# A hybrid decoder trunk: one pool per kind of tile, the second tokens' factors in the order of their products, and memory loaded earlier

## Chip, cores and metric

One NeuronCore of one Trainium2 chip runs the whole program in one launch. The metric is device time in microseconds (us) of that core. PE is TensorE, DVE VectorE, ACT ScalarE, POOL GpSimd, SP SyncE; in the rows a `q` behind an engine's name is its queue, where it issues DMAs or waits.

## What is computed

Two decoder layers over 512 tokens of width 1024, in float32, each of four steps with a layer norm (LN) behind every one. Layer 0 mixes with differential attention, layer 1 with a causal pooling mixer; both attend to 256 memory tokens.

```python
for i in range(DEPTH):                       # DEPTH = 2, a = 4 ** 0.25
    x = layer_norm(a * x + 0.5 * swiglu_ffn(x, ffn_w_in[i, 0], ffn_w_out[i, 0]), ...)
    h = diff_attention(x, ...) if i == 0 else pool_mixer(x, ...)
    x = layer_norm(a * x + h, ...)
    x = layer_norm(a * x + memory_cross_attention(x, mem, xa_wq[i], xa_wkv[i], xa_wo[i]), ...)
    x = layer_norm(a * x + 0.5 * swiglu_ffn(x, ffn_w_in[i, 1], ffn_w_out[i, 1]), ...)

def swiglu_ffn(x, w_in, w_out):              # D = 1024, D_FF = 2816
    g, u = jnp.split(x @ w_in, 2, axis=-1)
    return (jax.nn.silu(g) * u) @ w_out
```

In differential attention the output of a head is o = (p0 - lam p1) v, then scaled by the inverse root of its mean square plus a small constant; p0 and p1 are two softmaxes.

## The kernel before

Tokens lie in four tiles X of 128. Every float32 operand is split into a high and a low part: ACT casts the high one (`split`, line 111), DVE subtracts it for the low one (line 112), and `mm3` (lines 172 to 174) makes each product of three matmuls, hi x hi, hi x lo, lo x hi. Split weights are tiles wh (ACT) and wl (DVE) in the pool w; raw weights are loaded by SP into ra and rc (FFN) or raw (the other stages, two buffers).

An FFN multiplies 2x2 blocks with seven products instead of eight. `up` handles 256 of the 2816 columns of a half: its products x, y, z, then z and x again, use the factors of x in the order 0, 1, 3, 6, 4, 5, 2. Three such lanes run side by side in the first turn (`FFN_TURNS`), and two with a `down` beside them in the others. `more` (line 533) adds a further block to a raw tile by an accumulating DMA that POOL issues. Factors 0 and 1 are the transposed first 256 tokens, 2 to 6 are made from all 512: `turn_factors` (line 487) turns tokens 2 and 3 by PE and makes, a token at a time, s1 to s4 and the splits of factors 2 to 6 by half-width operations; the two sums of line 454 give it the first tokens back in one piece. `ffn` (line 427) traces it between the first x product and the y products.

Each stage ends with `to_tokens` or, in an FFN, `plain_down`: eight products over (half, token) in the order `LAST` (line 48), of which `summed` adds each to X and starts the LN of a token when its second half is in (`ln_token`, line 331: square on ACT, two small steps on POOL, two steps on DVE, lines 353 and 355). `TURNS` names the products behind which a finished token is already transposed for the next stage. The weights of `to_tokens` go to wh and wl, or, where `homes` is given, to activation tiles that have come free.

Each stage opens its pools anew: w, raw and one pool named phase for all activation tiles; six PSUM banks are a pool too (aux). A tile in a new pool waits for those older tiles whose addresses it covers. What the tile framework's scheduler puts in which order on an engine follows the order of tracing, unless `issue_after` or `high_priority` says otherwise. In differential attention `weave` (line 177) mixes the main stream (projections) with the side stream (scores, turns and outputs of heads); `da_out` (line 897) ends a head with four squares on ACT and five small steps on POOL. `load_memory` (line 1107) loads the memory into a raw tile, transposes it by 16 small matmuls and splits it; in layer 0 that is traced when cross-attention begins.

Of the kernel before, what the change touches and what calls it, by code (L numbers as in the profile page):

```python
# [17 lines left out]
P = 128  # L18
# [29 lines left out]
LAST = ((0, 0), (0, 1), (1, 0), (1, 1), (0, 2), (0, 3), (1, 2), (1, 3))  # L48
TURNS = ((0, 3), (1, 2))
# [52 lines left out]
class Trunk:  # L102
# [18 lines left out]
    def act(self, tag, shape=(P, S), dtype=F32R):  # L121

        return self.phase.tile(list(shape), dtype, tag=tag, name=tag, bufs=self.bufs[tag])
# [3 lines left out]

    @contextmanager
    def phase_pool(self, gain, spare, **bufs):

        self.gain, self.spare = gain, spare
        with self.tc.tile_pool(name="phase", bufs=1, reuse_waits="tile") as p:
            self.phase, self.bufs = p, bufs
            yield

    @contextmanager
    def stage_pools(self, raw, aux, w=5, order=("w", "raw")):


        pool = lambda name, **k: self.tc.tile_pool(name=name, bufs=1, reuse_waits="tile", **k)  # L140
        with ExitStack() as ctx:
            pools = {n: ctx.enter_context(pool(n)) for n in order}
            self.wp, self.rawp = pools["w"], pools["raw"]
            self.memp = pools.get("mem")
            self.auxp = ctx.enter_context(pool("aux", space=PSUM))
            self.w_bufs, self.raw_bufs, self.aux_bufs, self.aux_turn = w, raw, aux, 0
            yield

    def raw_tile(self, shape, tag="raw"):
        return self.rawp.tile([P] + list(shape), F32, tag=tag, name=tag, bufs=self.raw_bufs[tag])  # L150
# [4 lines left out]
    def aux(self, name, tag=None):  # L155
        if tag is None:
            tags = [t for t in self.aux_bufs if t != "yz"]
            tag = tags[self.aux_turn % len(tags)]
            self.aux_turn += 1
        return self.auxp.tile([P, S], F32, tag=tag, name=name, bufs=self.aux_bufs[tag])  # L160
# [55 lines left out]
    def hl(self, shape):  # L216
        return (
            self.wp.tile(shape, F32R, tag="wh", name="wh", bufs=self.w_bufs),
            self.wp.tile(shape, F32R, tag="wl", name="wl", bufs=self.w_bufs),
        )  # L220
# [110 lines left out]
    def ln_token(self, t):  # L331
# [20 lines left out]
        for i, c in enumerate(cols):  # L352
            nc.vector.scalar_tensor_tensor(y[i], X[:, c], mean, g[i], ALU.add, ALU.mult)
# [4 lines left out]
        self.ends.append((square, end))  # L358
        if t == NT - 1:
# [24 lines left out]
    def turn(self, t, half, two_pass=None):  # L384

        pt = self.aux("pt", "px" if "px" in self.aux_bufs else None).rearrange("p (c n) -> p c n", c=4)
# [8 lines left out]
        self.turned = self.split(hi[:, :, o], lo[:, :, o], pt)  # L395

# [30 lines left out]
    def ffn(self, layer, j, ln, beside=None):  # L427
# [22 lines left out]
        raw = [self.tmp("hb", (P, 4, 2 * P)) for _ in range(2)]  # L450
        act, dve = self.first_split
        with self.tc.issue_after(act.ins), self.tc.issue_after(dve.ins):
            for r, (hi, lo) in zip(raw, self.factors):
                self.nc.vector.tensor_tensor(r, hi.bitcast(F32), lo.bitcast(F32), ALU.add)
            self.turn_factors(2, raw)
        for w in works[1:]:
            next(w)
        self.turn_factors(3, raw)
        n = len(FFN_TURNS)
        for turn in range(n):  # L460
            behind = turn == n - 1
            for step in range(1 if turn == 0 else 0, 9 if behind else 7):
                if step == 4:
# [23 lines left out]
    def turn_factors(self, t, raw):  # L487


        nc, F = self.nc, self.factors  # L490
        o = slice(t % 2 * P, (t % 2 + 1) * P)
        pts = []
        for half in range(2):
            pt = self.aux("pt", (("py", "yz"), ("px", "py"))[t % 2][half])
            pt = pt.rearrange("p (c n) -> p c n", c=4)
            with self.behind():
                self.transpose4(pt, [self.X[t][:, half * S + j * P : half * S + (j + 1) * P] for j in range(4)])
            pts.append(pt)
        a11, a12 = (r[:, :, o] for r in raw)
        a21 = self.tmp("sr", (P, 4, P))  # L500
        nc.scalar.copy(a21, pts[0])
        s12, s34 = (self.tmp(f"b{i}", (P, 2, 4, P)) for i in ((1, 2) if t == 2 else (3, 4)))
        s1, s2, s3, s4 = s12[:, 0], s12[:, 1], s34[:, 0], s34[:, 1]
        part = lambda i, x: self.split(F[i][0][:, :, o], F[i][1][:, :, o], x)
        nc.vector.tensor_tensor(s1, pts[1], a21, ALU.subtract)
        part(3, s1)
# [358 lines left out]
    def da_scores(self, st, i):  # L865
# [4 lines left out]
        mx, sm, cf = self.small("mx"), self.small("sm"), self.small("cf", (P, 1))  # L870
        rc = st["rc"][:, i]
# [12 lines left out]
        nc.vector.reciprocal(rc, sm)  # L884
        nc.vector.scalar_tensor_tensor(cf, sm[:, 0:1], self.nlam, rc[:, 1:2], ALU.mult, ALU.mult)
# [11 lines left out]
    def da_out(self, st, i):  # L897
        nc = self.nc
        if i == 0:
            st["o"] = self.tmp("o", (P, NT, P))  # L900
# [480 lines left out]
```

## Time and profile before

| | us |
|---|---|
| median of 3 runs (lowest, highest) | 2035.2 (2034.3, 2036.3) |
| the profiled execution | 2036.3 |
| its span, first to last instruction | 2034.5 |
| busy in it: PE, DVE, ACT, POOL | 1966.0, 1575.2, 1019.3, 324.7 |

The stages follow one another in the span: FFN (0 to 345), differential attention (to 608), cross-attention (to 782), FFN (to 1132), FFN (to 1477), pooling mixer and cross-attention (to 1683), FFN (to the end). The profile page says how busy each engine is; a view of windows gives that for chosen stretches, with the clock granted to PE (1.00 is 2.4 GHz); a list of waits says who waited for whom; a timeline gives single instructions.

### The profile page before, as it was taken

The numbers are of one execution on the slowest core, as the hardware profiler recorded it, in microseconds if no ns is written. First come the engines' busy times: TensorE is split into PE (matmuls) and PEld (weight loads), VectorE is DVE, ScalarE is ACT, GpSimd is POOL, SyncE is SP. The second block draws the span as 40 slices with busy tenths as digits, with TensorE's granted clock in tenths as the row PEclk, the third lists the DMA queues.
The fourth block names the chain that finished last, engine by engine and source line by source line (L and its number), as shares of the span: only waits on it lengthen the run. The fifth ranks groups of instructions, "written<-read, shape, count | busy, mean of one in ns | idle before, by whom it ended". The sixth has DMA issues, their size and how long they took to land. (4 is left out here: it accounts for less than half of the span.)

```text
span 2034.5 us, 32534 instructions
## 1 busy us (share of the span) xinstructions
PE 1966.0 (97%) x13104; PEld 1804.7 (89%) x13104; DVE 1575.2 (77%) x2228; ACT 1019.3 (50%) x1553; POOL 324.7 (16%) x305
## 2 busy tenths in 40 slices
PE   8999999999998997999999899999989998999998
PEld 7999998887878987999998899999878888999996
DVE  7988887888866557688887878888787467888886
ACT  5555454566644435545553555455355435555452
POOL 2112121122110002211220311212000013111211
PEclk9999999999999998999999999999989999999999
DMA  9878772222115325977783677877253346777861
GB/s 260 175 164 177 166 135 83 84 65 83 63 42 175 116 67 140 188 166 157 145 183 118 139 163 165 177 164 147 74 166 125 104 114 136 152 163 164 180 138 44
DMA packets 246439, 277.96 MB, mean 137 GB/s; under 512 B 8208, under 2 KB 212496, under 8 KB 246288
## 3 DMA queue, kind: packets, MB, share of 16 engines
q0 software_dynamic: 92928, 92.29, 29.5%
q1 hardware_dynamic: 153360, 183.59, 27.8%
q8 instruction: 103, 1.69, 0.3%
q14 instruction: 48, 0.39, 0.1%
HBM read 273.75 MB, written 2.10 MB: 136 GB/s over the span
## 5 line engine op out<-in xcount | busy, mean ns | idle before, releaser
L533 POOL DMA_DIRECT2D ra<-in_ffn_w_in_dram x132 | 170.3, 1318 | 914.8 <-DVE wl L112 839.5
L111 ACT CAST wh<-ra 128x1024 fp32r<-128x1024 f32 x184 | 192.7, 1049 | 218.3 <-PE x L173 72.5
L112 DVE TENSOR_TENSOR wl<-ra,wh 128x1024 fp32r<-128x1024 f32 x184 | 223.8, 1224 | 83.3 <-ACT wh L111 83.3
L111 ACT CAST wh<-rc 128x1024 fp32r<-128x1024 f32 x136 | 142.5, 1049 | 158.2 <-PE x L173 43.9
L172 PE MATMUL x<-xh,wh 128*128 128x256 f32 x704 | 201.4, 286 | 5.6 <-ACT wh L111 5.6
L174 PE MATMUL x<-xh,wl 128*128 128x256 f32 x704 | 201.0, 285 | 3.5 <-DVE wl L112 3.5
L173 PE MATMUL x<-xl,wh 128*128 128x256 f32 x704 | 201.0, 285 | 0.8 <-DVE xl L112 0.8
L174 PE MATMUL x<-xe,wl 128*128 128x256 f32 x704 | 199.2, 283 | 0.0
L173 PE MATMUL x<-xe,wh 128*128 128x256 f32 x704 | 199.2, 283 | 0.0
L172 PE MATMUL x<-xe,wh 128*128 128x256 f32 x704 | 199.1, 283 | 0.0
L111 ACT CAST wh<-b 128x1024 fp32r<-128x1024 f32 x112 | 117.5, 1049 | 153.1 <-PE x L173 73.7
L112 DVE TENSOR_TENSOR wl<-rc,wh 128x1024 fp32r<-128x1024 f32 x136 | 165.3, 1223 | 37.2 <-ACT wh L111 37.2
L112 DVE TENSOR_TENSOR wl<-b,wh 128x1024 fp32r<-128x1024 f32 x112 | 137.1, 1224 | 50.8 <-ACT wh L111 50.3
L172 PEld LDWEIGHTS x<-xh,wh 128*128 128x128 f32 x704 | 136.7, 194 | 7.6 <-ACT wh L111 6.3
L174 PEld LDWEIGHTS x<-xh,wl 128*128 128x128 f32 x704 | 136.6, 194 | 4.0 <-DVE wl L112 4.0
L173 PEld LDWEIGHTS x<-xl,wh 128*128 128x128 f32 x704 | 136.7, 194 | 2.2 <-DVE xl L112 1.1
L173 PEld LDWEIGHTS x<-xe,wh 128*128 128x128 f32 x704 | 135.0, 192 | 1.2
L172 PEld LDWEIGHTS x<-xe,wh 128*128 128x128 f32 x704 | 135.0, 192 | 1.2
L174 PEld LDWEIGHTS x<-xe,wl 128*128 128x128 f32 x704 | 135.0, 192 | 0.0
L112 DVE TENSOR_TENSOR wl<-raw,wh 128x1024 fp32r<-128x1024 f32 x68 | 85.6, 1269 | 58.6 <-ACT wh L111 57.5
L350 POOL TENSOR_SCALAR var<-var 128x1 f32<-128x1 f32 x32 | 31.9, 996 | 507.5 <-ACT sp L349 248.9
L172 PE MATMUL z<-xh,wh 128*128 128x256 f32 x352 | 101.4, 288 | 10.8 <-DVE hr L578 4.8
(396 smaller groups left out, 6246.7 us busy)
## 6 DMA issues: line engine op xcount, KB each, us to landing
ra<-in_ffn_w_in_dram POOLq DMA_DIRECT2D x132, 512.0 KB, 6.7
rc<-in_ffn_w_in_dram SPq DMA_DIRECT2D x88, 512.0 KB, 4.9
b<-in_ffn_w_out_dram SPq DMA_DIRECT2D x76, 512.0 KB, 4.4
ra<-in_ffn_w_in_dram SPq DMA_DIRECT2D x44, 512.0 KB, 3.6
rc<-in_ffn_w_in_dram POOLq DMA_DIRECT2D x44, 512.0 KB, 8.8
raw<-in_xa_wkv_dram SPq DMA_DIRECT2D x16, 1024.0 KB, 5.4
raw<-in_da_w_qkv_dram SPq DMA_DIRECT2D x16, 512.0 KB, 5.0
raw<-in_xa_wq_dram SPq DMA_DIRECT2D x8, 1024.0 KB, 4.9
```

The lines of the kernel that those rows point to most:

```text
L111: self.nc.scalar.copy(hi, src),
L112: self.nc.vector.tensor_sub(lo, src, hi.bitcast(F32)),
L172: mm(out, w[0], x[0], start=start, stop=False, skip_group_check=again)
L173: mm(out, w[0], x[1], start=False, stop=False, skip_group_check=again)
L174: self.last_mm = mm(out, w[1], x[0], start=False, stop=stop, skip_group_check=again)
L350: nc.gpsimd.tensor_scalar(var, var, 1.0 / D, EPS * self.ln_scale**2, ALU.mult, ALU.add)
L533: nc.gpsimd.dma_start(t, source(*block), accum_op=ALU.add)
```

## The change

Every kind of tile gets its own pool, and each stage lists its pools in an order that fixes the layout. Of the PSUM pool three of two banks are made. The last four products of a stage change order. The second tokens' factors are made in the order 3 and 2 per token, then 6, then 4 and 5 for both tokens at once, and these steps are traced between the products. The last token's square and first LN step are queued behind the first weight split of an FFN. In differential attention the squares of two token tiles follow each pair, and the factor of a head takes its row sums in place of their inverses; the last weights go to tiles of qk, low and p. In layer 0 the memory is loaded into four tiles of p, with high priority.

```diff
-LAST = ((0, 0), (0, 1), (1, 0), (1, 1), (0, 2), (0, 3), (1, 2), (1, 3))
-TURNS = ((0, 3), (1, 2))
+LAST = ((0, 0), (0, 1), (1, 0), (1, 1), (0, 2), (1, 2), (0, 3), (1, 3))
+TURNS = ((1, 2), (0, 3))
...
+            self.phase = {t: ctx.enter_context(self.pool(t)) for t in bufs}
...
+            self.stage = {n: ctx.enter_context(self.pool(n)) for n in order}
+            self.banks = {n: ctx.enter_context(self.pool(n, space=PSUM)) for n in ("px", "py", "yz")}
...
+        self.begins = square, begin
...
-            self.turn_late(1 if (half, t) == TURNS[0] else 0)
+            self.turn_late(len(self.late) - 1)
...
+    def queue_behind(self, ins, first):
+        info = mybir.DependencyInfo(mybir.DependencyClass.NoSync, mybir.DependencyReason.DATA)
+        self.tc.add_manual_dep(ins.ins, first.ins.name, info, reason="queue_behind")
...
         act, dve = self.first_split
-        with self.tc.issue_after(act.ins), self.tc.issue_after(dve.ins):
-            for r, (hi, lo) in zip(raw, self.factors):
-                self.nc.vector.tensor_tensor(r, hi.bitcast(F32), lo.bitcast(F32), ALU.add)
-            self.turn_factors(2, raw)
+        if self.begins:
+            for late, first in zip(self.begins, (act, dve)):
+                self.queue_behind(late, first)
+        second = self.second_factors()
+        next(second)
         for w in works[1:]:
             next(w)
-        self.turn_factors(3, raw)
+        next(second)
...
             for step in range(1 if turn == 0 else 0, 9 if behind else 7):
+                if turn == 0 and step in (2, 3):
+                    next(second)
...
+    def second_factors(self):
+        nc, F, H = self.nc, self.factors, 2 * P
+        s1, s2, a21, s3 = (self.tmp(f"b{i}", (P, 4, H)) for i in range(1, 5))
...
+        for t in (2, 3):
...
+            nc.scalar.copy(a21[:, :, o], pts[0])
+            nc.vector.tensor_tensor(s1[:, :, o], pts[1], a21[:, :, o], ALU.subtract)
+            part(3, s1[:, :, o], o)
+            part(2, pts[1], o)
+            yield
+        raw = [self.tmp("hb", (P, 4, H)) for _ in range(2)]
+        for r, (hi, lo) in zip(raw, F):
+            nc.vector.tensor_tensor(r, hi.bitcast(F32), lo.bitcast(F32), ALU.add)
+        a11, a12 = raw
         nc.vector.scalar_tensor_tensor(s2, s1, -1.0, a11, ALU.mult, ALU.subtract)
+        s4 = s1
         nc.vector.scalar_tensor_tensor(s4, s2, -1.0, a12, ALU.mult, ALU.subtract)
         part(6, s4)
-        part(2, pts[1])
+        yield
         part(4, s2)
         nc.vector.tensor_tensor(s3, a11, a21, ALU.subtract)
         part(5, s3)
+        yield
...
+        sq = st["sq"]
+        for i in range(i - 1, i + 1):
+            nc.scalar.activation(
+                po[:, 0, 0], o[:, i], AF.Square, scale=float(P**-0.5), accum_out=sq[:, i : i + 1]
+            )
...
+        f, G, s0 = self.small("f", (P, NT)), nc.gpsimd, st["sm"][:, :, 0]
+        G.tensor_scalar(f, s0, EPS, None, ALU.mult)
+        G.tensor_tensor(f, f, s0, ALU.mult)
+        G.tensor_tensor(f, f, sq, ALU.add)
         G.tensor_tensor(f, f, self.mhalf, ALU.pow)
-        G.tensor_tensor(f, f, r0, ALU.mult)
...
+        homes = [[home("qk")] * 4, [home("low"), home("low"), home("p"), home("p")]]
+        drain(self.to_tokens(self.oT[4:], self.a["da_w_o"][0], 4, 4, False, True, ALPHA, homes))
...
+            raw = [[self.tmp(tag) for h in range(2)] for m in range(2)]
+            for m in range(2):
+                for h in range(2):
+                    nc.sync.dma_start(raw[m][h], src[:, m, h])
...
+                with self.phase_pool(("gb", "gb"), "p", pT=6, p=4, kv=8, **bufs):
+                    self.kvp = self.phase["kv"]
+                    with self.tc.high_priority():
+                        self.load_memory("p")
...
-        homes = [[q] * 4, [kv, kv, kv, pT]]
+        homes = [[lambda: self.pair("q")] * 4, [kv] * 4]
...
+        return self.stage_pools(4, dict(ra=4, rc=3), ("wh", "wl", "ra", "rc"))
+    def other_pools(self, order=("wh", "wl", "raw")):
+        return self.stage_pools(5, dict(raw=2), order)
...
+        bufs = dict(b1=1, b3=1, b2=1, b4=1, xe=6, hb=4, sp=4, ha=4, sr=1, hr=3)
...
+            bufs = dict(low=4, rt=2, a=4, p=4, o=1, qk=8, v=4, oT=11)
...
-            self.later.enter_context(self.other_pools(("raw", "mem", "w")))
+            self.later.enter_context(self.other_pools(("mem", "wl", "raw", "wh")))
+            bufs = dict(pw=1, pb=2, ps=2, ones=1, pooled=20, sq=1)
```

## Rows read from the trace of the kernel before

**Rows 1.** The page, part 1: busy us of PE, share of the span, instructions.
```profile
PE 1966.0 (97%) x13104; PEld 1804.7 (89%) x13104; DVE 1575.2 (77%) x2228; ACT 1019.3 (50%) x1553; POOL 324.7 (16%) x305
```
**Rows 2.** Windows: stretch, its length, each engine's busy us, granted clock, DMA share, GB/s.
```profile
580.00:625.00 45.00, 36.42 (x181) 30.70 (x180) 26.75 (x43) 16.51 (x33) 8.04 (x13) 0.89 0.34 113
780.00:825.00 45.00, 34.44 (x239) 32.76 (x238) 35.10 (x43) 25.36 (x37) 14.09 (x12) 0.85 0.86 199
1125.00:1165.00 40.00, 34.74 (x236) 32.53 (x235) 34.15 (x46) 22.38 (x34) 13.66 (x11) 0.91 0.68 153
1165.00:1425.00 260.00, 260.00 (x1909) 248.23 (x1908) 214.16 (x261) 134.72 (x164) 47.58 (x37) 1.00 0.77 163
1470.00:1500.00 30.00, 20.12 (x128) 18.64 (x126) 24.06 (x35) 14.73 (x23) 3.50 (x4) 0.77 0.69 230
1670.00:1715.00 45.00, 39.18 (x260) 36.01 (x259) 37.63 (x55) 24.18 (x37) 13.11 (x12) 0.92 0.50 117
```
**Rows 3.** PE's waits by releaser: us in total, times, the longest.
```profile
PE pk L172 <- ACT wh L111: 9.4, 1, 9.4
PE x L172 <- ACT wh L111: 5.6, 2, 4.8
...
PE z L172 <- DVE hr L578: 4.8, 4, 1.8
PE pv L172 <- ACT wh L111: 4.6, 1, 4.6
PE y L174 <- DVE wl L112: 4.0, 4, 1.2
PE x L174 <- DVE wl L112: 3.5, 2, 2.7
PE z L172 <- DVE xl L112: 3.1, 2, 1.6
...
PE pt L403 <- ACT o L929: 2.1, 1, 2.1
```
**Rows 4.** Windows on stretches at the lower clock.
```profile
584.80:588.20 3.40, 3.40 (x10) 2.56 (x11) 0.68 (x1) 1.42 (x4) 0.00 (x0) 0.50 0.00 0
...
1154.80:1161.70 6.90, 5.67 (x28) 5.51 (x27) 5.15 (x6) 0.89 (x2) 3.90 (x3) 0.51 0.76 213
1479.10:1492.80 13.70, 5.89 (x26) 5.60 (x27) 13.21 (x18) 7.98 (x12) 1.67 (x2) 0.50 0.73 243
```
**Rows 5.** An FFN's start: a window, then DVE's and PE's timeline (start, us, instruction).
```profile
1140.00:1156.00 16.00, 10.93 (x84) 9.96 (x82) 16.00 (x24) 12.51 (x21) 0.00 (x0) 0.96 0.41 131
...
1140.62 2.36 DVE L454 TENSOR_TENSOR hb<-xh,xl 128x1024 f32<-128x1024 f32 x2
...
1154.90 1.23 DVE L112 TENSOR_TENSOR wl<-rc,wh 128x1024 fp32r<-128x1024 f32 x1
...
1132.70 0.28 PE L172 MATMUL x<-xh,wh 128*128 128x256 f32 x1
1132.82 0.28 PE L173 MATMUL x<-xl,wh 128*128 128x256 f32 x1
```
**Rows 6.** Timeline of SP's queue and ACT at the FFN's start behind cross-attention.
```profile
757.62 0.37 SPq L529 DMA_DIRECT2D ra<-in_ffn_w_in_dram  x1
...
785.16 1.98 ACT L111 CAST wh<-ra 128x1024 fp32r<-128x1024 f32 x2
```
**Rows 7.** SP's waits from 560 to 640; ACT's timeline at 580 and 1485.
```profile
SPq L200 <- PE pt L1116: 30.2, 1, 30.2
...
580.31 0.28 ACT L917 ACTIVATE po<-o 128x128 f32<-128x128 f32 x1 [1.35 <-DVE o L912]
...
1485.35 3.88 ACT L111 CAST wh<-raw 128x1024 fp32r<-128x1024 f32 x4
```
**Rows 8.** The end: a window, and DVE's timeline.
```profile
2024.50:2034.50 10.00, 0.17 (x1) 0.00 (x0) 5.06 (x9) 1.24 (x2) 1.02 (x3) 0.71 0.28 106
...
2026.15 0.68 DVE L327 SCALAR_TENSOR_TENSOR X<-X,ps 128x512 f32<-128x512 f32 x1
```

More of the change, by code (lines that the diff above doesn't have):

```diff
@@ L121, in act, with pool, stage_pools @@
     def act(self, tag, shape=(P, S), dtype=F32R):
[L123 removed]
+        return self.phase[tag].tile(list(shape), dtype, tag=tag, name=tag, bufs=self.bufs[tag])
     def pair(self, tag, shape=(P, S)):
         return self.act(tag, shape), self.act(tag, shape)
+    def pool(self, name, **k):
+        return self.tc.tile_pool(name=name, bufs=1, reuse_waits="tile", **k)
     @contextmanager
     def phase_pool(self, gain, spare, **bufs):
[L131 to L133 removed]
+        self.gain, self.spare, self.bufs = gain, spare, bufs
+        with ExitStack() as ctx:
+            self.phase = {t: ctx.enter_context(self.pool(t)) for t in bufs}
             yield
     @contextmanager
[L137 to L140 removed]
+    def stage_pools(self, w, raw, order):
         with ExitStack() as ctx:
[L142 to L146, printed above, removed]
+            self.stage = {n: ctx.enter_context(self.pool(n)) for n in order}
+            self.banks = {n: ctx.enter_context(self.pool(n, space=PSUM)) for n in ("px", "py", "yz")}
+            self.w_bufs, self.raw_bufs, self.aux_turn = w, raw, 0
             yield
     def raw_tile(self, shape, tag="raw"):
[L150 removed]
+        return self.stage[tag].tile([P] + list(shape), F32, tag=tag, name=tag, bufs=self.raw_bufs[tag])
     def mm(self, name):
@@ L384, in turn @@
     def turn(self, t, half, two_pass=None):
-        pt = self.aux("pt", "px" if "px" in self.aux_bufs else None).rearrange("p (c n) -> p c n", c=4)
+        pt = self.aux("pt", "px" if "ra" in self.stage else None).rearrange("p (c n) -> p c n", c=4)
         c0 = half * S
@@ L485, in factor_tiles, with part @@
         return self.factor_views() + list(zip(new(), new()))
[L487 to L506, printed above, removed]
+    def second_factors(self):
+        nc, F, H = self.nc, self.factors, 2 * P
+        s1, s2, a21, s3 = (self.tmp(f"b{i}", (P, 4, H)) for i in range(1, 5))
+        def part(i, x, o=slice(0, H)):
+            self.split(F[i][0][:, :, o], F[i][1][:, :, o], x)
+        for t in (2, 3):
+            o = slice(t % 2 * P, (t % 2 + 1) * P)
+            pts = []
+            for half in range(2):
+                pt = self.aux("pt", (("py", "yz"), ("px", "py"))[t % 2][half])
+                pt = pt.rearrange("p (c n) -> p c n", c=4)
+                c0 = half * S
+                with self.behind():
+                    self.transpose4(pt, [self.X[t][:, c0 + j * P : c0 + (j + 1) * P] for j in range(4)])
+                pts.append(pt)
+            nc.scalar.copy(a21[:, :, o], pts[0])
[7 more added lines that the diff above has]
+        a11, a12 = raw
@@ L952, in da_main @@
                 k = self.da_key(k)
-                rc = self.small("rc", (P, NT, 2))
-                self.heads.append((self.clock, {"h": h, "q": q, "k": k, "v": vs, "rc": rc}))
+                sm = self.small("sd", (P, NT, 2))
+                self.heads.append((self.clock, {"h": h, "q": q, "k": k, "v": vs, "sm": sm}))
             if not vs:
@@ L1104, in pool_mixer, with load_memory @@
             self.ln_token(t)
-    def load_memory(self):
+    def load_memory(self, tag=None):
         nc = self.nc
-        raw = self.raw_tile((2, D))
-        nc.sync.dma_start(raw, self.a["mem"][0].rearrange("(m p) d -> p m d", p=P))
+        src = self.a["mem"][0].rearrange("(m p) (h d) -> p m h d", p=P, h=2)
+        if tag:
+            raw = [[self.tmp(tag) for h in range(2)] for m in range(2)]
+            for m in range(2):
+                for h in range(2):
+                    nc.sync.dma_start(raw[m][h], src[:, m, h])
+        else:
+            t = self.raw_tile((2, 2, S))
+            nc.sync.dma_start(t, src)
+            raw = [[t[:, m, h] for h in range(2)] for m in range(2)]
         self.memT = []
@@ L1115, in load_memory @@
                 for m in range(2):
-                    self.nc.tensor.transpose(
-                        pt[:, i, m], raw[:, m, (c + i) * P : (c + i + 1) * P], self.ident
-                    )
-            t = tuple(self.memp.tile([P, 2, MEM], F32R, name=f"mem{c}{n}") for n in "hl")
+                    o = (c + i) % 4 * P
+                    self.nc.tensor.transpose(pt[:, i, m], raw[m][c // 4][:, o : o + P], self.ident)
+            t = tuple(self.stage["mem"].tile([P, 2, MEM], F32R, name=f"mem{c}{n}") for n in "hl")
             self.split(t[0], t[1], pt.rearrange("p c m n -> p c (m n)"))
@@ L1241, in cross_attention @@
         else:
-            with self.later, self.phase_pool(("gb", "gb"), "p", **bufs):
+            with self.later, self.phase_pool(("gb", "gb"), "p", pT=6, p=4, **bufs):
                 self.xa(layer, ln)
@@ L1276, in run @@
             self.new_xt()
-            self.last_mm = None
+            self.last_mm = self.begins = None
             self.late, self.ln_next = list(range(NT)), "ffn"
```

49 lines of the change are left out of this document (15 added, 34 removed).

## The prediction

> **What bounds the kernel now.** I began with the page's busy times: TensorE (PE) works 1966.0 of 2034.5 us, so everything else together costs at most the 68.5 us in which it stands still, plus what its clock takes [rows 1]. The windows view says where that is. The long inside of an FFN has none of it: 260 of 260 us busy at a granted clock of 1.00, although VectorE (DVE) works 214 of these [rows 2]. The idle time sits where stages meet. As window minus PE busy: 8.6 us from differential attention to cross-attention (580 to 625), 10.6 at the next FFN's start (780 to 825), 5.3 between two FFNs (1125 to 1165), 9.9 where an FFN meets the pooling mixer (1470 to 1500), 5.8 at the last FFN's start (1670 to 1715) [rows 2]. The last 10 us are the tail, without PE [rows 8].
>
> The same rows show a granted clock of 0.77 to 0.92 there. A window laid on just the stretch at the lower level (1.2 GHz instead of 2.4) gives its price, half of PE's busy time in it: 1.7 us at 584.8, 2.8 at 1154.8, 2.9 at 1479.1 [rows 4]. There is one more like the first (in the first FFN) and four like the second (from 615.5, 786.2, 810.1 and 1704.4, at 2.0 to 2.9). Sum some 19.5 us. Each lies behind idle time or in it, so I let it go with the wait before it.
>
> Of PE's waits [rows 3], those of the z products (3.1 us on xl, 4.8 on hr) and of the y products (4.0 on wl) have one cause. DVE is busy 16.00 of 16 us from 1140 to 1156 [rows 5]: from the two sums of line 454 (2.36 us) at 1140.62 to the wl that y needs at 1154.90 lie 18 half-width factor operations and two hr, so (14.28 - 2.36) / 20 = 0.60 us each.
>
> **The change, part by part.** The sum is made against the profiled execution, 2036.3 us with 1.8 outside its span; the median of three is 2035.2, 1.1 lower, and I take the saving off the median.
>
> *Order of the factors (four FFN starts).* Factor 3, which z reads first, now comes straight from tokens 2 and 3: three half-width DVE operations a token, 6 x 0.60 = 3.6 us, where 2.4 + 18 x 0.60 = 13.2 stood ahead of y's and z's operands [rows 5]. The rest (two sums, s2, s4, s3, three splits, all 1024 wide at 2.36 / 2 = 1.18) is 9.4 us, traced after y and partly after the first z. A product advances PE by 0.12 us [rows 5]; x's three lanes of 24 take 8.6, y's as much, z's as much. Until factor 6 is due, 26 us after x's first product, DVE must do the last token's LN (some 3.5), 3.6, six wl at 1.23, three hr at 0.60 and, up to factor 6, 2.4 + 3 x 1.18 = 5.9: 22 us. It fits, so nothing new is late next. At 1125 to 1165 that saves 5.3 idle + 2.8 clock, of which I leave one wait of a wl (1.2) and 0.4: **6.5**. At the last FFN 5.8 + 2.8, less the same and half a us before x: **6.5**. In the first FFN two small waits and a clock stretch of 1.7 are at stake: **1.5**.
>
> *First split ahead of the last LN (780 to 825).* The first x waits 4.8 us on ACT's wh. The cast starts at 785.16, behind the last token's square in ACT's order, though its load was issued at 757.62; then x waits 2.7 for wl, behind LN on DVE [rows 6, 3]. The new order puts square and first LN step behind the split. What waits there then is the last token alone, due at the z products, 17 us after x begins. With the z and y waits, 10.6 idle and two clock stretches (2.0 + 2.9), 15.5 are at stake. SP's loads for lanes 1 and 2 find memory earlier in the new layout. I leave three waits of 1.2, one a lane: **12**.
>
> *Memory and weights of cross-attention (580 to 625).* SP waits 30.2 us, until the transposes of mem free a raw buffer, to load the next weights; PE waits 4.6 for their wh [rows 7, 3]. Now mem lies in four tiles of p and the last attention weights in qk, low and p, so raw, wh and wl come free for both loads. SP issues four loads for one, hidden, as it had only waits in these 30 us. At the head's end two of four squares and one of five POOL steps leave the chain on which PE waits 2.1 [rows 3]; between nothing and all of it goes, I take 1.6. At stake: 8.6 idle less the 0.5 kept of that, with clock 1.7 + 2.7, so 12.5. I leave one wait of 1.2 with its clock stretch, and half a us: **8**.
>
> *Pooling mixer (1470 to 1500).* pk waits 9.4 us for wh; the cast runs at 1485.35, behind a split of the last token in ACT's order [rows 3, 7]. The layout puts raw over tiles that an FFN frees early and wh over rc and b, away from the gain rows that LN reads to its end. At stake 9.9 + 2.9; how much goes depends on ACT's order, which the diff does not state: between 0 and 12.8. I take **8**, nearer the upper end, as load and buffer no longer hang on the last products, and leave the mem splits (four at 0.60) and most of the clock stretch.
>
> *LN order (LAST, TURNS).* Token 2's LN starts one product earlier, the last token's no earlier; but at the tail its add came at 2026.15, behind token 2's LN, while PE had ended 0.2 us after 2024.5 [rows 8]: **1.5**. The price: half 0's weights are held until the seventh of eight products instead of the sixth, so the next stage's splits have one product less of room in wh and wl.
>
> *The rest.* ACT waits 1.35 us for DVE before a head's squares [rows 7]; now it does so twice a head: from 0 (other heads fill it) to 8 x 1.35 = 10.8. Home splits are four half-width for two wide ones. Extra PSUM pools rotate the same six banks: nothing. With the later wh and wl I take **3** off, nearer 0: of PE's waits on ACT only the 2.1 lies in that stage [rows 3].
>
> Sum: 6.5 + 6.5 + 1.5 + 12 + 8 + 8 + 1.5 - 3 = 41. 2035.2 - 41 = **1994**.
>
> Two half-width operations (2 x 0.60) cost DVE what one wide one does (1.18) [rows 5], and every z product reads the columns of both tokens, so a half that is ready early lets nothing start. The Trainium skill ("Perfetto Trace Analysis", section "Optimizing Scalar/DVE Operations") advises against such joining: where Vector is not saturated but makes bubbles elsewhere, smaller pieces may finish the work sooner. By that page factor 6 would come three half-steps later, 1.8 us a start, an estimated 7 us in four, and the sum would be 34 (2001).
>
> **Rivals.**
> *The memory parts do not act* (the order on ACT and SP keeps casts or loads late): of 8 + 8 only the head's end stays (1.6 + 1.7), 12.7 lost: 2007. For it: the cast at 1485.35 is late by ACT's order. Against: SP's 30.2 us is plainly a buffer [rows 7]. Chance 0.20.
> *DVE still bounds the FFN starts*: the wait moves from z to y or to factor 6. The 14.5 of three starts vanish and the 12 falls to the 7.5 of x's two waits [rows 3]: 41 - 19 = 22, so 2013. For it: 16.00 of 16 us busy [rows 5]. Against: 22 of 26 us. Chance 0.13.
> *Nothing comes of it*: the engines keep their order, 2035. Chance 0.04.
> *Slower*: DVE, in order, gets the wide chain (9.4 us) ahead of y's and z's weight splits, and at the other two places wl behind LN. It decides from where y's second wl starts later than 14 us after x's first product (x's lanes, y's first and some slack). Then each start idles some 9.5 us, for which the row at 1470 gives 9.9 + 2.9 = 12.8; four make 51 against the 34 that they cost now, nothing is gained at the two others, the tail gives 1.5, the rest costs 3: 2035 + 18 = 2053. For it: wl stands behind the chain now [rows 5]. Against: y is traced ahead of the wide part. Chance 0.05.
> *Better*: no wait that I left survives, some 61 at stake: 1974. Chance 0.03.
>
> **Numbers.** The forecast has 0.55. The range takes it with its bounds and the two partial cases, 1980 to 2014, and leaves out about 0.15. A measurement of this kernel can tell about 0.2% (4 us) from no change. Faster by more: 0.55 + 0.20 + 0.13 + 0.03 = 0.91; same 0.04; slower 0.05.
>
> **What would show it.** Right: PE idle down to some 43 us and its busy time to some 1950; z's waits on xl and hr gone at all starts; clock 1.00 around 1150 and 1700; each FFN's first wh<-ra ahead of the last square; no weight load behind mem's transposes. Wrong: DVE full with PE waiting at y or z as before, a wait of several us on pk, SP held by mem's loads, or new waits on sc and po inside attention.

## The result, and the profile after

The changed kernel takes **1998.45 us** (median of 4 runs, 1997.66 to 1999.95) where the kernel before, in the same rounds, takes 2035.28 (4 runs, 2034.29 to 2036.34): a ratio of 0.982, 95% interval 0.9803 to 0.9837. The forecast was 1994, with a range from 1980 to 2014; it was 4.5 us too low. The profiled execution has a span of 1995.9 us, 38.6 less than before, and the rest of this text works on the two spans.

First the page of the changed kernel, part 1, as in [rows 1]:

```profile
PE 1952.4 (98%) x13104; PEld 1786.5 (90%) x13104; DVE 1567.7 (79%) x2208; ACT 1014.8 (51%) x1545; POOL 321.7 (16%) x297
```

PE has the same 13104 matmuls, with 13.6 us less of busy time (2034.5 - 1966.0 = 68.5 us idle before, 43.5 after, so 25.0 less of idle time). Busy time that falls with the same work is clock: of the eight stretches at the lower level ahead of the tail, the profiled execution of the changed kernel has one left.

Next the windows view of the changed kernel, on the stretches of [rows 2] moved to where the same work now lies (columns as there), then the one stretch at the lower clock, then the last 10 us:

```profile
582.00:627.00 45.00, 42.50 (x254) 36.23 (x254) 32.50 (x50) 22.32 (x38) 9.10 (x10) 1.00 0.33 105
770.00:815.00 45.00, 45.00 (x360) 43.99 (x360) 38.58 (x47) 28.07 (x39) 16.39 (x15) 1.00 0.64 138
1104.00:1144.00 40.00, 39.87 (x310) 38.43 (x309) 37.49 (x43) 27.44 (x38) 16.60 (x14) 1.00 0.76 158
1144.00:1404.00 260.00, 258.74 (x1882) 245.66 (x1881) 215.10 (x265) 132.50 (x161) 43.78 (x34) 1.00 0.77 163
1436.00:1466.00 30.00, 24.85 (x140) 21.53 (x139) 25.96 (x39) 14.95 (x25) 5.88 (x6) 0.94 0.47 142
1636.00:1681.00 45.00, 44.03 (x325) 41.47 (x324) 42.37 (x53) 29.50 (x42) 15.34 (x16) 1.00 0.54 112
1985.90:1995.90 10.00, 2.03 (x9) 1.33 (x8) 3.86 (x9) 1.24 (x2) 0.74 (x2) 0.80 0.25 94
1455.90:1459.30 3.40, 3.40 (x18) 3.40 (x17) 2.93 (x4) 1.12 (x3) 1.70 (x1) 0.51 0.94 302
```

Idle time of PE (window minus busy) went from 8.6 to 2.5, from 10.6 to 0, from 5.3 to 0.1 and from 5.8 to 1.0 at four of the five places, and the clock is 1.00 there. At the pooling mixer 5.2 of 9.9 us stay, with the one stretch at half clock (1.7 us). The long inside of an FFN, which had no idle time, now has 1.3 us.

PE's waits in the changed kernel, the longest (as [rows 3]):

```profile
PE pt L408 <- DMA X<-in_x_dram: 5.5, 1, 5.5
PE z L173 <- DVE wl L112: 3.0, 3, 2.6
PE sc L894 <- DVE a L112: 1.8, 2, 1.4
PE x L171 <- DVE hr L618: 1.8, 2, 1.2
PE ps L171 <- DVE X L326: 1.7, 2, 1.1
PE pt L1149 <- DVE X L326: 1.7, 1, 1.7
```

The waits of pk (9.4), x and pv on wh and of z on hr and xl are off this part of the list; the longest that is left is that for the first load of x, which no part of the change touches. One sign that the prediction counted as wrong is there, though small: scores in attention (sc) wait 1.8 us for DVE's low part of an operand, where it was 0.6.

The table gives the gain by stretches, from points read off the two timelines (the start or end of a named PE operation: x is the first product of an FFN, py one of its `down`, v a value product of attention, xq a query product of cross-attention, pk and pv its keys and values of the memory), beside the term of the prediction:

| stretch | before | after | gain | predicted |
|---|---|---|---|---|
| start to the first FFN's last py | 288.7 | 289.1 | -0.4 | 1.5 |
| to the last v (attention) | 257.5 | 259.6 | -2.1 | nothing (bound 10.8 lost) |
| to cross-attention's first xq | 86.0 | 76.4 | 9.6 | 8 |
| to the first py of the FFN behind it | 241.7 | 227.1 | 14.6 | 12 |
| to the next FFN's first x | 258.8 | 259.4 | -0.6 | |
| to its first py | 85.4 | 77.8 | 7.6 | 6.5 |
| to its last py | 192.9 | 193.7 | -0.8 | |
| to cross-attention's last xq (mixer) | 214.7 | 210.4 | 4.3 | 8 |
| to the last FFN's first py | 141.8 | 136.3 | 5.5 | 6.5 |
| to its last py | 192.9 | 193.7 | -0.8 | |
| to the end | 74.1 | 72.4 | 1.7 | 1.5 |

The gains sum to 38.6. The five negative rows (-4.7 in all, 2.6 of it inside the FFNs and their ends) stand against the 3 that the prediction took off for "the rest".

### The profile page after: what moved, and what is told of

It reads as the page before. It is cut to its first block, busy times and chain, and to the rows that moved or that the text cites. A ratio compares the mean times of both kernels' runs of the same rounds, so it can differ in the third digit from the quotient of the medians.

```text
span 1995.9 us, 32504 instructions
## 1 busy us (share of the span) xinstructions
PE 1952.4 (98%) x13104; PEld 1786.5 (90%) x13104; DVE 1567.7 (79%) x2208; ACT 1014.8 (51%) x1545; POOL 321.7 (16%) x297
## 3 DMA queue, kind: packets, MB, share of 16 engines
q0 software_dynamic: 92928, 92.29, 30.2%
## 5 line engine op out<-in xcount | busy, mean ns | idle before, releaser
L112 DVE TENSOR_TENSOR wl<-raw,wh 128x1024 fp32r<-128x1024 f32 x64 | 80.7, 1266 | 53.7 <-ACT wh L111 52.8
L173 PE MATMUL z<-xh,wl 128*128 128x256 f32 x352 | 99.7, 285 | 2.8 <-DVE wl L112 2.8
L111 ACT CAST wh<-raw 128x1024 fp32r<-128x1024 f32 x64 | 66.6, 1050 | 70.1 <-PE xq L172 21.5
```

The costliest lines, as they stand in the source:

```text
L111: self.nc.scalar.copy(hi, src),
L112: self.nc.vector.tensor_sub(lo, src, hi.bitcast(F32)),
L173: self.last_mm = mm(out, w[1], x[0], start=False, stop=stop, skip_group_check=again)
```

## Experiments

Each kernel was timed in three rounds beside the kernel before; "before" was 2035.8 to 2036.6 us in them. What an edit costs is said against the changed kernel's 1998.45, and placed by the same points of the timeline. The interval of the changed kernel's ratio is 0.0017 wide to each side, some 3.4 us, so less than that is no difference. Where two intervals overlap, the sum does not tell the kernels apart, and a place in the timeline is the reading of one profiled execution.

### The order of the factors

**Old factors in the changed kernel.** The queueing behind the first split stays.

```diff
-        second = self.second_factors()
-        next(second)
+        raw = [self.tmp("hb", (P, 4, 2 * P)) for _ in range(2)]
+        with self.tc.issue_after(act.ins), self.tc.issue_after(dve.ins):
+            ...
+            self.turn_factors(2, raw)
...
-        next(second)
+        self.turn_factors(3, raw)
```

> The kernel after, with the factors of tokens 2 and 3 made as before (a token at a time, all factors, traced between the x products). If the order of the factors is what freed the FFN starts, z waits on xl and hr and y on wl come back at all four starts, with the lower clock behind them: 15 to 22 us slower than after (about 2014 to 2020), the two later starts 6 to 8 us each. The rival is that token 2's earlier LN and the earlier loads had already freed VectorE there, and the factors' order only rode along: under 6 us slower (under 2004).

Measured: 2011.78 us (ratio 0.9879, 0.9864 to 0.9894), 13.3 slower. The loss lies between each FFN's first x and its first py (at the last FFN counted from the last xq): 6.8, 4.5 and 5.7 us at the three FFNs behind another stage, nothing at the first. That is below the range of the theory and far over the rival. z waits for hr again (first line; PE's waits of this kernel, lines as in [rows 3]):

```profile
PE z L171 <- DVE hr L586: 4.7, 4, 1.8
PE z L173 <- DVE wl L112: 3.7, 2, 1.8
PE y L173 <- DVE wl L112: 1.9, 2, 1.2
```

**New factors alone in the kernel before.**

```diff
-        self.turn_factors(3, raw)
+        next(second)
...
+                if turn == 0 and step in (2, 3):
+                    next(second)
```

> The kernel before with one part alone: factor 3 straight from tokens 2 and 3, then 2, then 6, 4 and 5 over both tokens at once. Taken out of the changed kernel this part was worth 13.3 us (4.5 to 6.8 at each of three FFN starts). Theory: it acts by itself at the two starts that follow an FFN or cross-attention, so it gains 12 to 18 us on the kernel before: 2017 to 2023. Rival: it needs the earlier weights that the layout gives, because in the old layout y and z wait for wh and wl anyway; then it gains under 7: 2028 to 2035.

Measured: 2017.94 us (0.9913, 0.9898 to 0.9928), 18 us faster than before, as the theory had it. At the two starts that the prediction put at 6.5 each the first py comes 7.7 and 6.9 us sooner; behind cross-attention it gains 3.5, and there x still waits for its weights. The window on the start between two FFNs in this kernel, then its longest waits on weights:

```profile
1122.00:1162.00 40.00, 40.00 (x313) 38.81 (x312) 37.06 (x42) 25.66 (x36) 16.31 (x15) 1.00 0.79 159
...
PE pk L172 <- ACT wh L111: 9.4, 1, 9.4
PE x L172 <- ACT wh L111: 5.9, 3, 4.8
PE x L174 <- DVE wl L112: 5.8, 2, 5.1
...
PE pv L172 <- ACT wh L111: 4.8, 1, 4.8
```

40 of 40 us at full clock where it was 34.74 at 0.91 [rows 2]: this part needs nothing else. The waits of pk, pv and x on weights are those of before [rows 3]; they belong to the other parts.

### The order of the last products

```diff
-LAST = ((0, 0), (0, 1), (1, 0), (1, 1), (0, 2), (1, 2), (0, 3), (1, 3))
-TURNS = ((1, 2), (0, 3))
+LAST = ((0, 0), (0, 1), (1, 0), (1, 1), (0, 2), (0, 3), (1, 2), (1, 3))
+TURNS = ((0, 3), (1, 2))
...
-            self.turn_late(len(self.late) - 1)
+            self.turn_late(1 if (half, t) == TURNS[0] else 0)
```

> The kernel after, with the last four products of a stage in the old order. If token 2's earlier LN gives room on VectorE at each stage's end, the tail is 1.5 to 1.8 us longer and the FFN starts lose about 1 us each: 3 to 6 us slower. The rival is that the weights held one product longer cost more than that where the next stage needs wh, wl or the memory's place (pooling mixer, differential attention): then those two places gain 2 to 4 us and the whole is within 2 us of after, or faster.

Measured: 1990.79 us (0.9776, 0.9761 to 0.9791), 7.7 us **faster** than the changed kernel, with intervals that don't touch. The tail loses 1.4 from PE's last product on, but nearly every place where another stage follows gains (0.4 is lost between the last v and the first xq): 1.5 up to the last v, 1.0 at the FFN behind cross-attention, 1.8 between two FFNs, 2.0 up to the mixer's last xq, 2.2 at the last FFN. ACT's timeline where two FFNs meet shows why (a row `sp<-X,mean` is the square of a token, a row `xh<-pt` the high part of a token that PE has just transposed), first the changed kernel:

```profile
1096.16 1.15 ACT L348 ACTIVATE sp<-X,mean 128x1024 bf16<-128x1024 f32 x1 [4.28 <-DVE mean L335]
...
1103.24 1.16 ACT L348 ACTIVATE sp<-X,mean 128x1024 bf16<-128x1024 f32 x1
...
1104.39 1.05 ACT L111 CAST wh<-ra 128x1024 fp32r<-128x1024 f32 x1
1107.26 1.08 ACT L111 CAST xh<-pt 128x512 fp32r<-128x512 f32 x2 [1.82 <-PE pt L408]
1108.22 2.01 ACT L111 CAST wh<-ra 128x1024 fp32r<-128x1024 f32 x2
```

and the same with the old order:

```profile
1094.28 1.15 ACT L348 ACTIVATE sp<-X,mean 128x1024 bf16<-128x1024 f32 x1 [4.28 <-DVE mean L335]
...
1095.43 1.04 ACT L111 CAST wh<-ra 128x1024 fp32r<-128x1024 f32 x1
1100.40 1.08 ACT L111 CAST xh<-pt 128x512 fp32r<-128x512 f32 x2 [3.93 <-PE pt L408]
1101.36 2.01 ACT L111 CAST wh<-ra 128x1024 fp32r<-128x1024 f32 x2
...
1107.50 1.15 ACT L348 ACTIVATE sp<-X,mean 128x1024 bf16<-128x1024 f32 x1 [1.05 <-DVE mean L335]
```

Counted from the square of token 1 (1096.16 and 1094.28), the next FFN's first weight cast comes 8.23 us behind it in the new order and 1.15 in the old, so 7.1 later, and the next two 5.0 later (12.06 against 7.08). The first one stands behind the square of token 2, which now comes a product earlier (a token's LN takes its place in ACT's and DVE's order). The next two stand behind the cast of the token that PE transposes after half 0's last product; that product is the last to read half 0's wh, and its last matmul on it starts 5.0 later too (1106.39 and 1099.5). The second is what the prediction named as the price of the reorder; the first it did not see. The two were not separated by a run.

### The start behind cross-attention, and the layout

**No queueing behind the first split.**

```diff
-        if self.begins:
+        if False:
```

> The kernel after, without queueing the last token's square and first LN step behind the first weight split. If that order is what removed x's 4.8 and 2.7 us waits at the start of layer 0's second FFN, they come back there with a stretch at the lower clock: 7 to 10 us slower (2005 to 2008), and nothing changes at the other starts. The rival is that the layout, by which the loads come earlier, removed them: within 2 us of after.

Measured: 1997.73 us (0.9818, 0.9796 to 0.9839): no difference, and none over 0.2 us between the first xq and the next FFN's first py. The queueing does nothing. ACT's timeline of the changed kernel shows that it had nothing to do:

```profile
756.29 1.05 ACT L111 CAST wh<-ra 128x1024 fp32r<-128x1024 f32 x1 [6.11 <-DMA ra<-in_ffn_w_in_dram]
...
760.79 1.05 ACT L111 CAST wh<-ra 128x1024 fp32r<-128x1024 f32 x1 [1.90 <-DMA ra<-in_ffn_w_in_dram]
761.75 1.05 ACT L111 CAST wh<-rc 128x1024 fp32r<-128x1024 f32 x1
762.70 1.14 ACT L348 ACTIVATE p<-X,mean 128x1024 bf16<-128x1024 f32 x1
...
780.20 1.15 ACT L348 ACTIVATE p<-X,mean 128x1024 bf16<-128x1024 f32 x1
```

Four casts, all three lanes' first (from ra) and lane 0's for y (from rc), run ahead of the square of any token (the first at 762.70, the last token's at 780.20), and the first three waited for their loads alone. Before, the first cast came at 785.16, behind the last token's square, and SP issued the fourth load at 779.38 [rows 6 show the first], which is issued at 751.23 now. In the next two kernels, which have an older layout, all three casts from ra keep ahead of the squares (the first at 757.22 and 767.03), while the first cast from rc, lane 0's for y, comes at 782.53 and 797.49, against 761.75 in the changed kernel: what these layouts delay is the weights of y, not those of lanes 1 and 2. The first cast is ahead of the squares in every run that keeps all or part of the new layout, and behind them (784.55) where the new factors alone stand in the kernel before. So the layout is what is left as the cause, by elimination; no run undoes all of it, and which detail brought the first cast forward was not isolated.

**The pools in the old order**, one per kind of tile still.

```diff
-        bufs = dict(b1=1, b3=1, b2=1, b4=1, xe=6, hb=4, sp=4, ha=4, sr=1, hr=3)
+        bufs = dict(hr=3, sr=1, sp=4, b1=1, b2=1, b3=1, b4=1, xe=6, ha=4, hb=4)
...
-            bufs = dict(low=4, rt=2, a=4, p=4, o=1, qk=8, v=4, oT=11)
+            bufs = dict(v=4, qk=8, low=4, rt=2, p=4, a=4, o=1, oT=11)
...
-            self.later.enter_context(self.other_pools(("mem", "wl", "raw", "wh")))
+            self.later.enter_context(self.other_pools(("raw", "mem", "wh", "wl")))
```

> The changed kernel with its pool per kind of tile, but the pools listed in the old order of the tiles in every stage (and raw, mem, wh, wl for the pooling mixer). Theory: the order of the pools decides which old tiles a new one waits for, so the loads and splits of an FFN behind cross-attention and of the pooling mixer come later again: 8 to 15 us lost, 2006 to 2013, with some 4 us of it at the FFN start from 776 us and some 4 at the pooling mixer from 1450 us. Rival: having separate pools is what matters, and their order little: 1997 to 2001.

Measured: 2003.57 us (0.984, 0.9824 to 0.9857), 5.1 slower; the intervals overlap, so the sum is a likely one. The profiled execution is 7.2 longer: 2.5 us up to the first xq, 4.7 from there to the first py behind cross-attention (6.5 from the FFN's first x, which comes 1.8 sooner), 3.6 at the mixer's pk, and some 4 given back elsewhere. These are the theory's places, but the loss is below its range of 8 to 15. ACT's cast of the third lane's first weights and its first from rc in this kernel, at the FFN behind cross-attention:

```profile
760.79 1.05 ACT L111 CAST wh<-ra 128x1024 fp32r<-128x1024 f32 x1 [1.00 <-DMA ra<-in_ffn_w_in_dram]
...
782.53 1.05 ACT L111 CAST wh<-rc 128x1024 fp32r<-128x1024 f32 x1
```

**One pool for all activation tiles.**

```diff
-            self.phase = {t: ctx.enter_context(self.pool(t)) for t in bufs}
+            p = ctx.enter_context(self.pool("phase"))
+            self.phase = {t: p for t in bufs}
```

> The changed kernel with one pool for all activation tiles of a stage again, as before; wh, wl, ra, rc and raw keep pools of their own. The old order of the pools alone cost 7.2 us of span: 6.5 at the FFN start behind cross-attention, 2.5 at the first q product and 3.6 at the pooling mixer, with some of it given back later. Theory: it is the order of the activation tiles that counts for the FFN start (its ra, rc and weights cover tiles of cross-attention), and a joined pool loses that order: 2002 to 2007, with 4 to 7 us lost from 776 to 852 us. Rival: the places of the weight and raw tiles carry it: under 2 us lost, 1997 to 2001.

Measured: 2020.06 us (0.992, 0.9906 to 0.9935), 21.6 slower, well past the theory. The FFN start behind cross-attention loses 4.8 from its first x to its first py, as expected (3.0 counted from the first xq); what was not expected is 13.1 at cross-attention's first xq, and 8.2 at the mixer's pk, of which 3.9 is back by the last xq. PE's waits and SP's timeline of this kernel:

```profile
PE pt L1150 <- DMA p<-in_mem_dram: 13.4, 1, 13.4
PE pk L172 <- ACT wh L111: 7.7, 1, 7.7
...
572.83 5.26 SPq L200 DMA_DIRECT2D raw<-in_xa_wkv_dram  x2
611.05 0.37 SPq L200 DMA_DIRECT2D raw<-in_xa_wq_dram  x1
613.44 0.37 SPq L200 DMA_DIRECT2D raw<-in_xa_wkv_dram  x1
613.86 2.03 SPq L1139 DMA_DIRECT2D p<-in_mem_dram  x4
```

In the changed kernel the four memory loads are issued at 578.87; here at 613.86, behind a weight load (611.05) for which SP waited 32.9 us. So four loads on SP that the prediction called hidden cost 13 us here: the high priority is no help in a queue in which something else waits first. Whether their own tiles would have been free sooner the trace does not show. These 13 us hang on the joined pool together with the memory in tiles of p (the kernel before had it in a raw tile); a joined pool with the memory in a raw tile was not run.

**wh and wl in one pool, ra and rc in another, the mixer's pools as before.**

```diff
+            for t, n in (("wh", "w"), ("wl", "w"), ("ra", "raw"), ("rc", "raw")):
+                if n in self.stage:
+                    self.stage[t] = self.stage[n]
...
-        return self.stage_pools(4, dict(ra=4, rc=3), ("wh", "wl", "ra", "rc"))
+        return self.stage_pools(4, dict(ra=4, rc=3), ("w", "raw"))
...
-            self.later.enter_context(self.other_pools(("mem", "wl", "raw", "wh")))
+            self.later.enter_context(self.other_pools(("raw", "mem", "w")))
```

> The changed kernel with wh and wl in one pool again, ra and rc in another, and the pooling mixer's pools in the order raw, mem, w as before; the activation tiles keep their own pools in the new order. Theory: the mixer's early memory loads and casts need this part: its stretch loses 3 to 8 us (1383 to 1594 us of the span) and the FFN starts under 2: 2002 to 2009. Rival: the activation pools carry both places: under 2 us lost, 1997 to 2001.

Measured: 1996.47 us (0.9805, 0.9789 to 0.9821): no difference. The mixer's pk comes 3.2 us later and waits 3.7 for wh, but 1.8 of that is back by the last xq:

```profile
PE pk L174 <- ACT wh L111: 3.7, 1, 3.7
```

It is the rival: pools of their own for the activation tiles carry what the layout gives, those for the weight and raw tiles nothing that can be measured while the activation pools stay.

### Memory and the last weights of attention

**Memory in a raw buffer, without priority.**

```diff
-                    with self.tc.high_priority():
-                        self.load_memory("p")
+                    self.load_memory()
```

> The kernel after, with layer 0's memory loaded into a raw tile as before, without priority. If the raw buffer was what SP waited 30 us for, the load of the second weights again waits for the memory's transposes, and TensorE waits 4 to 6 us with 2 to 3 us of clock at 600 to 625: 6 to 9 us slower (2004 to 2008). The rival is that the last weights' new places alone freed raw early enough: within 2 us of after.

Measured: 2000.74 us (0.9818, 0.9801 to 0.9834), so not to be told from the changed kernel; from the last v to the first xq it loses 0.4 us. (Its profiled execution, with a span of 2005.9, lost 3.0 us ahead of the last v and 8.4 at the mixer, which the edit does not touch; see the last section.) The theory falls.

**The last attention weights in wh and wl.**

```diff
-        drain(self.to_tokens(self.oT[4:], self.a["da_w_o"][0], 4, 4, False, True, ALPHA, homes))
+        drain(self.to_tokens(self.oT[4:], self.a["da_w_o"][0], 4, 4, False, True, ALPHA))
```

> The changed kernel with one part undone: the last weights of differential attention go to wh and wl again, not to tiles of qk, low and p. Theory: it is these homes that carry the gain of 9.6 us between the last attention head and the first q product of cross-attention, because wh and wl are free when the first weights of the memory's keys arrive (their casts at 599.4 and 607.4 us in the changed kernel, 607.8 and 613.0 before); where the memory is loaded to added only 0.4 us there. Then it is 6 to 10 us slower than the changed kernel: 2004 to 2009, with the loss between 549 and 632 us of the span. Rival: either of the two parts alone is enough, so this too loses under 2 us: 1998 to 2001.

Measured: 1999.81 us (0.9827, 0.9811 to 0.9844), no difference, with 1.8 us at the first xq. The rival: neither part alone is needed.

**Both undone**, as the two diffs above.

> The changed kernel with both memory parts undone: no tiles of qk, low and p for the last weights of differential attention, and the memory in a raw buffer without priority. Alone they cost 1.8 us (homes) and 0.4 us (memory) between the last attention head and the first q product of cross-attention, of the 9.6 us that the change gained there. Theory: each covers for the other, since either brings one weight load of the memory's keys forward; with both gone the wait for the values' weights (4.6 us before) and its clock stretches come back: 6 to 9 us slower than the changed kernel, 2004 to 2008. Rival: the sum of the two, 2 to 3 us, since it is the pools and their order that carry the rest (the old order alone cost 2.5 there): 2000 to 2002.

Measured: 2003.81 us (0.9843, 0.9826 to 0.9861), 5.4 slower, with 5.7 at the first xq, against 0.4 + 1.8 for each alone. The interval just overlaps that of the changed kernel, so it is the place that speaks. PE's waits of this kernel from 578 to 630, then ACT's first two casts for the memory's keys (599.37 and 607.39 in the changed kernel, 607.77 and 613.03 before):

```profile
PE pk L173 <- DVE wl L213: 3.9, 1, 3.9
...
608.06 1.05 ACT L211 CAST wh<-raw 128x1024 fp32r<-128x1024 f32 x1
...
613.98 1.04 ACT L211 CAST wh<-raw 128x1024 fp32r<-128x1024 f32 x1
```

A wait comes back, 3.9 us of the keys' product on wl where before it was 4.6 of the values' on wh, with a stretch of 6.8 us at half clock at 614.4. So the parts cover for each other, as the theory said, just short of its range. Of the 9.6 us, 5.7 hang on them; against the rest stand the 2.5 of the old order of the pools and the 1.2 of the old squares (next).

**The squares of a head at its end**, as before.

```diff
-        sq = st["sq"]
-        for i in range(i - 1, i + 1):
...
+        for i in range(NT):
+            nc.scalar.activation(po[:, 0, 0], o[:, i], AF.Square, accum_out=sq[:, i : i + 1])
```

> The changed kernel with the squares of a head as before: all four at its end, with five steps on GpSimd and the inverse row sums. The prediction took 1.6 us of gain at the end of the last head, and a possible loss of up to 10.8 us inside attention. In the changed kernel attention is 2.2 us longer than before up to the last value product, and 1.5 of that went away with the old order of the last products. Theory: the squares cost at most 0.7 inside and gain 1 at the end (the wait of the last head's turns on its scaled output was 2.1 us before and 1.1 after): 1997 to 2000, not to be told from the changed kernel. Rival: the squares cost the 2.2 us inside attention: 1995 to 1997.

Measured: 1997.54 us (0.9815, 0.9800 to 0.9830), no difference: 0.1 us faster up to the last v, 1.2 lost from there to the first xq. The squares behind each pair cost nothing inside attention (of the bound of 10.8 none), and the 2.1 us lost there came with the order of the last products (1.5).

### Put together

The old order of the products in all stages but the last, where the new one stays, and in layer 1 the memory's transposes in PSUM banks of px and mm.

```diff
-LAST = ((0, 0), (0, 1), (1, 0), (1, 1), (0, 2), (1, 2), (0, 3), (1, 3))
+LAST = ((0, 0), (0, 1), (1, 0), (1, 1), (0, 2), (0, 3), (1, 2), (1, 3))
+END = LAST[:5] + ((1, 2), (0, 3), (1, 3))
...
-        for n, (half, t) in enumerate(LAST):
+        for n, (half, t) in enumerate(END if self.last_ln else LAST):
...
-            pt = self.aux("pt").rearrange("p (c m n) -> p c m n", c=2, m=2)
+            pt = self.aux("pt") if tag else self.mm("pt") if c % 4 else self.aux("pt", "px")
+            pt = pt.rearrange("p (c m n) -> p c m n", c=2, m=2)
```

> Three parts put together: the changed kernel; the old order of the last products in every stage but the last (worth 7.7 us where it stood in all of them, of which the tail gave 1.4 back, which the new order in the last stage alone should keep); and in layer 1 the transposes of the memory in PSUM banks of px and mm, which an FFN's end leaves free, where they waited 1.7 us for the last sums with py and yz. Theory: 1.4 better at the tail and 1 to 4 at the pooling mixer than 1990.8: 1985 to 1989. Rival: at the mixer DVE's LN chain sets the time and not the banks, so only the tail moves: 1989 to 1990.

Measured: 1989.32 us (0.9776, 0.9760 to 0.9793), the fastest of all: 9.1 us faster than the changed kernel, not to be told from 1990.79. The tail keeps its 1.4, as the rival too had it. At the mixer PE no longer waits for a bank, but now 2.7 us for the cast of a token that the LN has just finished (PE's waits of this kernel, then DVE's last LN step of that token and ACT's cast behind it):

```profile
PE pp L1098 <- ACT xh L112: 2.7, 1, 2.7
...
1454.31 1.28 DVE L355 SCALAR_TENSOR_TENSOR X<-X,rstd,sr 128x1024 f32<-128x1024 f32 x1
...
1455.88 1.13 ACT L112 CAST xh<-X 128x512 fp32r<-128x512 f32 x2
```

The LN step ends at 1455.59, the cast follows at 1455.88 and the product at 1456.55: DVE's chain of LNs sets the time there, and the banks stood in front of it.

## Why the prediction held, step by step

**The sum.** 38.6 us of span against 41, and the reading behind it held: idle time where stages meet, with the clock falling behind it. Six of the eight stretches at half clock went with their waits, and that at the mixer shrank. The eighth, in the first FFN, is missing by chance of the profiled execution: z waits longer there than before, and eleven of the twelve kernels above have a stretch of 3.4 to 6.8 us at that place again.

**Order of the factors** (6.5 + 6.5, and 1.5). Right in mechanism and size: 7.6 and 5.5, and 7.7 and 6.9 alone. DVE is still busy 16.00 of 16 us at the start (1119 to 1135), but PE now 15.87 of these (10.93 before [rows 5]), since what y and z need comes first: the rival in which DVE goes on bounding these starts is out. The first FFN gained nothing; instead of one wait of 1.5 us z now has one of 2.6 for wl.
That the later factors are made from both tokens at once cost at most the new waits of x on hr (1.8 in all, 0.7 with the old order of the last products). The Trainium skill ("Perfetto Trace Analysis", section "Optimizing Scalar/DVE Operations") says that breaking up instructions may let work end sooner where Scalar or Vector are not saturated but make bubbles on other engines; by that the prediction's sum was 34. No product waits for DVE's part of factor 4, 5 or 6 (tiles xe) in the list of waits, so the 7 us of that sum do not show. The whole saving, 36.8 us, does not decide between 34 and 41, and no run made these factors half-width in the new order.

**First split ahead of the last LN** (12). The size held (14.6; the factors alone give 3.5 of it, and cost 5.8 when taken out of the changed kernel), the mechanism did not: the step "the new order puts square and first LN step behind the split" did nothing. What is left for the cause is the layout, of which the prediction had one clause (SP's loads for lanes 1 and 2 find memory earlier): the old order of the pools costs 4.7 there, with y's weights late, and the rest was not isolated. Where a cast stood behind a square in ACT's order, I took the instruction that imposes an order for the cause of the new one; with the new pools the cast is ahead without it. That the size came out is luck.

**Memory and weights of cross-attention** (8; 9.6 came). The prediction's sentence "raw, wh and wl come free for both loads" named SP's 30.2 us as what counts. With the memory in raw again the second load is issued at 613.79, later than before (610.58, the end of the wait in [rows 7]), and PE loses 0.4: the late load cost almost nothing by itself while wh and wl were free.

**Pooling mixer** (8; 4.3 came). The mis-sized term. The loads are early (1415 for 1467) and the wait of 9.4 is gone, but the transposes wait for banks, then the mem splits, and behind both DVE's LNs; from the other side, joined weight pools bring a wait of 3.7 back at a net cost of some 1.4. Early weights are worth only what the LN chain leaves. Of the 3.7 that are missing, 2.0 went to the order of the last products: with the old one this stretch gains 6.3.

**LN order** (1.5). The tail gave it (DVE's last add at 1987.97 waits for PE alone, where it stood behind token 2's LN before [rows 8]):

```profile
1987.97 0.69 DVE L326 SCALAR_TENSOR_TENSOR X<-X,ps 128x512 f32<-128x512 f32 x1 [1.94 <-PE ps L173]
```

But "one product less of room in wh and wl", priced within the 3 for all the rest, cost together with the earlier square, which the prediction did not see, 9 us in the other stages. This is the step that failed in sign: the reorder is a net loss of 7.7, and without it the kernel is at 1990.8. The forecast came so near in part by luck: this miss and that at the mixer stood against gains somewhat larger than taken elsewhere.

**The rivals.** "The memory parts do not act": half of it happened, at the mixer only. "Slower" did not: y's weights are split in time (y waits 0.9 us for wl in all, 4.0 before [rows 3]).

## What to carry to other kernels

Ask of every tile of a new stage which late tile it covers: joining the pools of the activation tiles again cost 21.6 us here (13 of it through the memory's loads), while joining those of the weights made no difference. A load of high priority is no help behind a load that waits in the same queue. When a token's LN is started earlier, look at what stands behind it in the next stage's order and how long the weights are held; a reorder that helps the tail can cost at every other stage end, and may be used at the tail alone. Two parts that bring the same operand forward cover for each other, so undoing one shows little: undo both.

## What was not expected of the hardware

The clock can fall for longer behind the same waits. With the memory in raw the profiled execution has the same waits at the mixer as the changed kernel (1.7, 1.4 and 0.9 us the longest), yet PE ran 17.1 us at the lower level behind them, where the changed kernel ran the same stretch at full clock. First that kernel, then the changed one (windows):

```profile
1466.40:1483.50 17.10, 17.10 (x84) 17.10 (x82) 10.95 (x15) 6.72 (x10) 0.00 (x0) 0.50 0.28 86
```
```profile
1465.20:1482.30 17.10, 17.10 (x147) 17.01 (x147) 14.55 (x23) 10.07 (x16) 0.00 (x0) 1.00 0.55 173
```

PE is busy in both to the full, with 84 matmuls in one and 147 in the other, and 8.4 us are gone: being busy for all of 17.1 us did not bring the full clock back sooner. The four runs of that kernel lie between 1997.4 and 2007.7, so what it costs differs from run to run; why it fell is left open.
